# Storing the first tile of a gated linear unit by rows instead of in one piece

## The chip, the cores and the metric

The kernel runs on one core of a Trainium2 chip. The metric is device time in microseconds (us) of one launch. Before the change it is 933.2 us. A timed run is called slow when it lies over 1.5% above the fastest of the same kernel; the others are called fast.

## The reference

```python
def reference(x):                       # x: 8192 x 8192, float32
    a, b = np.split(x, 2, axis=-1)
    return a * (1 / (1 + np.exp(-b)))   # 8192 x 4096, float32
```

It reads 268 MB, writes 134 MB, and does one sigmoid and one product per output element.

## The kernel before

The matrix is cut into 32 tiles of 256 rows; each of the 128 partitions holds two neighbouring rows. There are two input slots (64 KB per partition each) and two output slots (32 KB each). SyncE issues one load per tile, ScalarE takes the sigmoid in place, VectorE multiplies into the output slot, and ScalarE issues the store. Only the first and the last tile are computed in quarters: row 0's two halves, then row 1's.

```python
    for i in range(n_tiles):
        ...
        load = nc.sync.dma_start(out=xs[i % SLOTS], in_=x_t[i])
        ...
        if 0 < i < n_tiles - 1:
            parts = [(slice(0, R), slice(0, half))]
        else:
            w = half // 2
            parts = [
                (slice(r, r + 1), slice(c * w, (c + 1) * w)) for r in range(R) for c in range(2)
            ]
        ...
        for k, (r, c) in enumerate(parts):
            b = rows[:, r, 1, c]
            sig = nc.scalar.activation(out=b, in_=b, func=SIG)
            mul = nc.vector.tensor_mul(out=packed[:, r, c], in0=rows[:, r, 0, c], in1=b)
            ...
            by_sigmoid = i % 2 == 1 and len(parts) == 1
            implied(mul, *(s for s in old["stores"] if by_sigmoid or s not in freed))
            if by_sigmoid:
                for s in freed:
                    tc.add_manual_dep(sig.ins, s.ins.name, DEP, reason="frees the output slot")
            ...
            if i == n_tiles - 1 and k > 0:
                store(chunks[k - 1])
        store(chunks[-1] if i == n_tiles - 1 else slice(0, R * half))
```

The words that follow: a DMA engine moves data between HBM (the main memory) and SBUF (the memory on the chip), and a core has 16 of them. By the traces' packet records, each of the 16 moves eight packets of 64 KB of a load and eight of 32 KB of a store, and then one *semaphore packet* of 4 bytes; when all 16 of these are through, the transfer has landed and the instruction that waits for it may start. A *ring* is the list of packets that loads, or stores, have waiting on an engine; it runs empty when the next transfer is issued too late.

`implied` takes away a dependency that follows from others. `freed` are the stores that must have landed before the output slot is written again: tile k waits for store k-2. In odd tiles the sigmoid does this waiting (`by_sigmoid`), in even ones the product.

## Time and profile before

| What | Value | Where from |
|---|---|---|
| time, median of 3 runs | 933.2 us (933.03 to 933.31) | timed runs |
| span of the profiled run | 931.7 us | page |
| one tile of 8.39 MB in and 4.19 MB out | 29.0 us | loads' semaphore packets in the trace |
| ScalarE per tile, VectorE per tile | 7.03 us, 8.69 us | groups of instructions |

A tile needs 29.0 us of the DMA engines and 15.7 us of computing, which lies beside other transfers. The windows view has one line per stretch (from:to, length, busy time and count of each engine, granted clock, share of the DMA engines, GB/s); its line for 200 to 490 us of the kernel before gives the steady rate:

```profile
200.00:490.00 290.00, 86.95 (x11) 70.31 (x10) 0.00 (x0) 1.00 1.00 434
```

The waits view (who waited for what: us in total, times, longest) of the kernel before has no wait for a store at all; the input is always what comes last:

```profile
ACT x_sb L68 <- DMA x_sb<-in_x_dram: 694.4, 32, 22.3
DVE o_sb L69 <- ACT x_sb L68: 647.1, 33, 23.9
```

### The profile page before, as it was taken

The page shows a single profiled execution, that of the slowest core. Times are in us where ns is not written, and L with a number is a line of the kernel's source. Part 1 is how long each engine was busy: PE and PEld are TensorE (multiplying, and loading weights), DVE is VectorE, ACT ScalarE, POOL GpSimd, SP SyncE. Part 2 cuts the span into 40 slices and gives each one's busy share as a digit, 9 for nine tenths or more (in the row PEclk, how much of TensorE's full clock was granted, in tenths as well). Part 3 has the DMA queues.
Part 4 walks back from the last instruction along what each step waited for, and adds up shares of the span by engine and source line. Part 5 has one row for each costly group of instructions (what it writes and reads, how often), then busy time and mean ns, then how long its engine had stood idle before and what let it go on. Part 6 is the DMA issues. An engine that isn't in the chain of part 4 may idle for free.

```text
span 931.7 us, 247 instructions
## 1 busy us (share of the span) xinstructions
DVE 278.7 (30%) x38; ACT 227.1 (24%) x39; POOL 0.2 (0%) x4
## 2 busy tenths in 40 slices
DVE  0333213333133331233312333123331233312333
ACT  1323330233311333113331133311333113332033
POOL 0000000000000000000000000000000000000000
DMA  9999999999999999999999999999999999999999
GB/s 405 428 450 428 422 456 405 450 428 428 450 418 438 428 436 442 428 428 450 447 408 428 442 459 428 413 460 411 450 428 425 453 408 447 428 428 450 425 430 405
DMA packets 9649, 402.67 MB, mean 432 GB/s; under 512 B 1072, under 2 KB 1072, under 8 KB 1072
## 3 DMA queue, kind: packets, MB, share of 16 engines
q1 hardware_dynamic: 4608, 268.44, 66.6%
q10 hardware_dynamic: 5040, 134.22, 33.4%
q14 instruction: 1, 0.01, 0.0%
HBM read 268.44 MB, written 134.22 MB: 432 GB/s over the span
## 4 chain that ended last, share of the span: by engine, by line
DMA 73%; DVE 15%; ACT 12%; issue 0%; ACTq 0%
DMA x_sb<-in_x_dram 73%; DVE o_sb L69 15%; ACT x_sb L68 12%; ACTq L62 0%; ACTq L68 0%
## 5 line engine op out<-in xcount | busy, mean ns | idle before, releaser
L69 DVE TENSOR_TENSOR o_sb<-x_sb 128x8192 f32<-128x8192 f32 (+1 forms) x38 | 278.7, 7344 | 647.1 <-ACT x_sb L68 647.1
L68 ACT ACTIVATE x_sb<-x_sb 128x8192 f32<-128x8192 f32 (+1 forms) x38 | 225.8, 5952 | 695.6 <-DMA x_sb<-in_x_dram 694.4
L68 ACT ACT_TABLE_LOAD x1 | 1.3, 1283 | 0.8 <-PEq L188 0.8
L188 POOL MEMSET const-bfloat16-1.0<- 128x1 bf16 x1 | 0.1, 102 | 0.0
L188 POOL MEMSET const-uint8-127<- 128x1 uint8 x1 | 0.1, 102 | 0.0
L188 POOL MEMSET const-float32-0.0<- 128x1 f32 x1 | 0.1, 99 | 0.2 <-issue 0.2
L188 POOL MEMSET const-float32-1.0<- 128x1 f32 x1 | 0.1, 99 | 0.0
## 6 DMA issues: line engine op xcount, KB each, us to landing
out_dram<-o_sb ACTq DMA_DIRECT2D x31, 4096.0 KB, 34.7
out_dram<-o_sb ACTq DMA_DIRECT2D x4, 1024.0 KB, 5.6
x_sb<-in_x_dram SPq DMA_DIRECT2D x32, 42.2
```

Source lines behind the costliest of these rows:

```text
L68: sig = nc.scalar.activation(out=b, in_=b, func=SIG)
L69: mul = nc.vector.tensor_mul(out=packed[:, r, c], in0=rows[:, r, 0, c], in1=b)
L188: nc = _bacc.Bacc("TRN2", target_bir_lowering=False, num_devices=1)
```

## The change

The intent is to start storing earlier: row 0 of the first tile leaves as soon as its two products are done.

```diff
             if i == n_tiles - 1 and k > 0:
                 store(chunks[k - 1])
-        store(chunks[-1] if i == n_tiles - 1 else slice(0, R * half))
+            if i == 0 and r.start > 0 and c.start == 0:
+                store(slice(0, half))
+        if i == 0:
+            store(slice(half, R * half))
+        else:
+            store(chunks[-1] if i == n_tiles - 1 else slice(0, R * half))
```

## The prediction

> **What bounds the kernel now.** I read the page's slices first, then its queues and DMA issues, then the chain of waits, then the timeline of the first two tiles, and last the DMA view of one tile's time in the middle.
>
> ```profile
> DVE  0333213333133331233312333123331233312333
> ACT  1323330233311333113331133311333113332033
> ...
> DMA  9999999999999999999999999999999999999999
> ...
> q1 hardware_dynamic: 4608, 268.44, 66.6%
> q10 hardware_dynamic: 5040, 134.22, 33.4%
> ...
> HBM read 268.44 MB, written 134.22 MB: 432 GB/s over the span
> ...
> DMA x_sb<-in_x_dram 73%; DVE o_sb L69 15%; ACT x_sb L68 12%; ACTq L62 0%; ACTq L68 0%
> ...
> out_dram<-o_sb ACTq DMA_DIRECT2D x31, 4096.0 KB, 34.7
> out_dram<-o_sb ACTq DMA_DIRECT2D x4, 1024.0 KB, 5.6
> x_sb<-in_x_dram SPq DMA_DIRECT2D x32, 42.2
> ```
>
> The compute engines are busy in one to three tenths of each slice; the 16 DMA engines in nine tenths or more of every one, the first and the last included. The two queues' packet times add up to 66.6 + 33.4 = 100% of the engines' span. So the time is bytes over rate: 402.66 MB at 432 GB/s is 932 us. The chain of waits gives 15% to VectorE and 12% to ScalarE, and it would be easy to read 27% to be won there; but while those instructions run, the DMA engines move the other slot's load and the previous store. The chain tells which event released which, not which resource was short.
>
> The timeline of the start shows what the change touches:
>
> ```profile
> 21.95 7.31 ACT L68 ACTIVATE x_sb<-x_sb 128x2048 f32<-128x2048 f32 x4 [19.89 <-DMA x_sb<-in_x_dram]
> 23.89 8.90 DVE L69 TENSOR_TENSOR o_sb<-x_sb 128x2048 f32<-128x2048 f32 x4 [23.89 <-ACT x_sb L68]
> 32.82 0.38 ACTq L62 DMA_DIRECT2D out_dram<-o_sb  x1
> 44.80 7.03 ACT L68 ACTIVATE x_sb<-x_sb 128x8192 f32<-128x8192 f32 x1 [15.53 <-DMA x_sb<-in_x_dram]
> 51.86 8.69 DVE L69 TENSOR_TENSOR o_sb<-x_sb 128x8192 f32<-128x8192 f32 x1 [19.07 <-ACT x_sb L68]
> 60.58 0.36 ACTq L62 DMA_DIRECT2D out_dram<-o_sb  x1
> ```
>
> Load 1 was issued at the start, right behind load 0, so it streams from 21 to 44 us whatever the store does. There is no hole for an earlier store to fill. In the windows view, 0 to 33 us (loads alone) moves 413 GB/s with the start-up in it, and 45 to 103 us (both kinds) 434 GB/s.
>
> In the middle, 129 to 158 us, the DMA view says:
>
> ```profile
> DMA packets 288, 12.58 MB, mean 434 GB/s; under 512 B 32, under 2 KB 32, under 8 KB 32
> ...
> q1 hardware_dynamic: 144, 8.39, 66.7%
> q10 hardware_dynamic: 144, 4.19, 33.5%
> ```
>
> In 29 us exactly one load and one store pass. Per engine that is 8 data packets of 64 KB and 8 of 32 KB, and one small semaphore packet each. The packet records give 2.42 us for a 64 KB packet, 1.21 for 32 KB and 0.31 for 8 KB: the time goes with the bytes, with almost nothing fixed per packet. 8 x (2.42 + 1.21) = 29.0 us. Read engine by engine, they alternate strictly: a load packet, a store packet; a semaphore packet takes a turn too.
>
> **What the Trainium skill says.** "DMA: Bandwidth & Descriptors", section "Queues, rings and completion order", says that each DMA engine goes round-robin between the queue rows that have work, packet by packet. The trace agrees (144 against 144 packets). Its "Specifications" give a fabric ceiling of 435 GB/s; the 434 GB/s measured here sits at it, so nothing that reorders transfers can raise the rate. "Perfetto Trace Analysis", section "DMA Optimizations", says that splitting DMAs may help "If DMA engines are generally idle"; here they are not, so by that page the split has nothing to win.
>
> **The change part by part.**
> 1. *Issue times.* Sigmoids are 1.9 us and multiplies 2.29 us each. The second product ends at 23.89 + 2.29 + 2.2 = 28.4 us; row 0's store is issued at 28.4 instead of 32.8, 4.4 us earlier. It stands in ScalarE's order after the third sigmoid (done at 27.5) and before the fourth, which now starts near 28.8 instead of 27.4 and ends at 30.7. The fourth product starts then instead of at 30.5: row 1's store and load 2 leave at about 33.1, 0.25 us later. Load 2 isn't needed before load 1 has landed at 44, so this costs nothing.
> 2. *Packets.* Store 0 becomes 16 packets of 16 KB per engine (estimate from the row above: 0.61 us) for 8 of 32 KB, and one more semaphore packet (0.009 us in the records). 16 x 0.61 - 8 x 1.21 is under 0.1 us. Sum: +0.1 us.
> 3. *Turns.* This is the part that really moves something. While store 0 is in flight, a round is 2.42 + 0.61 = 3.03 us instead of 3.63: the load still gets a full 64 KB turn, the store only 16 KB. Before, the store's first packet came 6 us after its issue (38.9; the engine finished its current load packet and the next, which was stretched from 2.4 to 3.3 us). With the same lag the first 16 KB packet comes at 34.0. Then load 1's last three packets take turns with it: 34.0 + 3 x 3.03 + 0.61 = 43.7 us for load 1's semaphore, the same as now (43.7): two turns of 32 KB or four of 16 KB have gone in between. Load 1 lands at 44.8 in both. Store 0 has then 11 packets of 16 KB left. Load 2's eight rounds cost 8 x 3.03 = 24.2 us, so it lands near 68.9 instead of 73.65. Load 3 meets three more 16 KB turns and one semaphore turn, then four 32 KB ones: its semaphore at 94.6 and landing at 95.5 instead of 102.8. The loads run ahead by 7 us, and the stores fall behind by the same bytes.
> 4. *The new wait.* Store 0's last semaphore falls at 80.1 (landing 81.0); the third tile's product, ready at 75.9, waits for its output slot and ends at 89.7 (now 89.4). Store 1, issued at 60.6, gets its first turn at 82.5 and its last semaphore at 109.1, landing at 110.0 instead of 95.3. Tile 3 is odd: its sigmoid waits for store 1. It starts at 110.1, 14 us after its load has landed, and load 5 and store 3 go out at 110.1 + 7.03 + 8.69 = 125.9, where now it is 118.7. Load 4 is through at 122.5, so the load ring is empty for about 4 us. In that time the store ring still holds three or four packets of store 2, until 128.5. Load 5's packets can come from 126.9 (one microsecond after issue, as for the first load). So the DMA engines stay busy, with 1.6 us in hand; the loads fall back by those store packets.
> 5. *Afterwards.* I followed the turns to tile 7: store k-2 lands about 3.6 us after load k, odd tiles wait for it that long, and both rings always hold work. 29.0 us per tile as before.
> 6. *The end.* Some 4 store packets per engine more are left when the last load has landed (4 x 1.21 = 4.8 us), and that load is earlier by about the same. Now the last quarter's store is issued at 925.8, and the store queue works without a gap until 930.8. After the change the compute tail of 11 us (925.8 - 914.7) starts near 910 and ends near 921, while stores keep the engines busy to the same end.
>
> Sum: +0.1 us of packets, and a waking load ring at 126 us, which may stretch a packet by up to 0.9 us as the first store's did. I take half of that: +0.5 us. 933.2 + 0.5 = 933.7.
>
> **The rivals.**
> A. *The earlier store shortens the kernel by its 4.4 us* (0.5%), 928.8. For it: the chain has the first tile's compute in it. Against: no slice is idle, so 4.4 us would need a rate above 434 GB/s.
> B. *The slot wait drains both rings.* Step 4 has only 1.6 us in hand at 126 us; if the store's queue runs out first, or the wait recurs as a bubble at each odd tile, the cost is 1 to 3 us once (936), or 15 times 1 us (948). Against the recurrence: after the first time 5 to 8 store packets are left whenever a load is issued late.
> C. *The small packets cost.* 16 KB at half the efficiency would add 10 us x 1 = 10 us. Against: 8 KB packets take 0.31 us, a quarter of the 32 KB time.
> D. *The late tail.* If the last tile's products waited for store 29, the last stores would be late. One packet of it is left then, 1.2 us plus about 1 us to land; the first sigmoid takes 1.9 us. No cost.
>
> **Range and chances.** The three runs before span 0.3 us. Downward I see only spread, 0.5 to 1 us. Upward there are B's single bubble and differences between chips: 932.7 to 935.3. Two per cent are 18.7 us; only a recurring bubble with much more than 1 us per odd tile would reach it: 0.01 for slower, 0.005 for faster.
>
> **What would show it right or wrong.** Right: row 0's issue near 28.4; 144 packets more in q10 and 100% of DMA time; load 2 landing near 69 and load 3 near 95.5; a new line in the waits, ScalarE's sigmoid (or VectorE's product) released by a store, near 3 to 4 us per odd tile with one of 14; the store's median landing longer than 34.7 by some 10 us; the last sigmoid near 910. Wrong: DMA digits under 9 near 126 us or at the end, a period other than 29.0 us, or load landings that don't move. A faster time with unchanged DMA rate would sink the whole reading.

## The result

| | median | runs |
|---|---|---|
| before | 933.23 us | 6 runs, 933.03 to 933.78 |
| changed | 935.51 us | 933.74, 933.99, 934.19, 936.83, 941.03, and one slow run of 960.4 |

The ratio of the fast runs is 1.0027 (95% interval 1.0006 to 1.0048). Such a ratio is the mean time of one kernel's fast runs over that of the other's of the same rounds, so it isn't quite the ratio of the medians. It is a small loss, 0.2 us outside my range. The median of 935.51 takes in the slow run: that of the five fast ones is 934.19, inside my range, and that of all nine fast runs, with those of the repeat below, 935.44. More striking than its size is the spread: the six runs of the kernel before lie within 0.8 us, the five fast ones of the changed kernel within 7.3 us.

From the page of the changed kernel (the profiled run took 936.83 us, span 935.4), the lines that answer to those of before:

```profile
DMA  9999999999999999999999999999999999999998
...
q1 hardware_dynamic: 4608, 268.44, 66.6%
q10 hardware_dynamic: 5184, 134.22, 33.3%
...
out_dram<-o_sb ACTq DMA_DIRECT2D x30, 4096.0 KB, 42.2
out_dram<-o_sb ACTq DMA_DIRECT2D x2, 2048.0 KB, 39.3
out_dram<-o_sb ACTq DMA_DIRECT2D x4, 1024.0 KB, 8.1
```

The store queue has its 144 packets more (5184 instead of 5040) and still the same share of the time, so the smaller packets cost nothing that shows. The stores take 42.2 us from issue to landing instead of 34.7, and the last four 8.1 instead of 5.6.

The timeline of the changed kernel (start, length, engine, instruction; in brackets what ended the idle time before it):

```profile
28.49 0.37 ACTq L62 DMA_DIRECT2D out_dram<-o_sb  x1
...
33.18 0.36 ACTq L62 DMA_DIRECT2D out_dram<-o_sb  x1
45.98 7.03 ACT L68 ACTIVATE x_sb<-x_sb 128x8192 f32<-128x8192 f32 x1 [15.16 <-DMA x_sb<-in_x_dram]
...
70.16 7.03 ACT L68 ACTIVATE x_sb<-x_sb 128x8192 f32<-128x8192 f32 x1 [17.15 <-DMA x_sb<-in_x_dram]
82.36 8.69 DVE L69 TENSOR_TENSOR o_sb<-x_sb 128x8192 f32<-128x8192 f32 x1 [20.62 <-DMA out_dram<-o_sb]
...
111.20 7.03 ACT L68 ACTIVATE x_sb<-x_sb 128x8192 f32<-128x8192 f32 x1 [34.01 <-DMA out_dram<-o_sb]
...
126.99 0.36 ACTq L62 DMA_DIRECT2D out_dram<-o_sb  x1
```

Row 0 leaves 4.3 us earlier than the whole store did. The third tile's product (82.36) and the fourth tile's sigmoid (111.20) now wait for a store. The waits view says the same for the whole run:

```profile
ACT x_sb L68 <- DMA x_sb<-in_x_dram: 357.7, 17, 22.0
ACT x_sb L68 <- DMA out_dram<-o_sb: 327.3, 14, 34.0
DVE o_sb L69 <- DMA out_dram<-o_sb: 20.6, 1, 20.6
```

Where the time went in this run shows in the windows view of the changed kernel:

```profile
120.00:128.00 8.00, 6.96 (x1) 0.60 (x1) 0.00 (x0) 1.00 1.04 451
128.00:146.00 18.00, 8.69 (x1) 6.42 (x1) 0.00 (x0) 1.00 1.00 402
146.00:900.00 754.00, 223.29 (x26) 182.75 (x26) 0.00 (x0) 1.00 1.00 434
...
931.00:935.40 4.40, 0.00 (x0) 0.00 (x0) 0.00 (x0) 1.00 0.39 166
```

Between 128 and 146 us the rate is 402 GB/s (18 us x 32/434 = 1.3 us lost) with the DMA share still at 1.00: packets took longer, and no engine stood idle. After 931 us the engines are on average only 39% busy: some are done and others aren't.

The packet records show both. They don't name the engine, so I put packets into 16 sequences by letting each start where another ended. One of them, in the changed kernel (start, L = load or S = store with KB, or sem for a semaphore packet, length):

```
120.10 L64 2.42 | 122.51 S32 1.21 | 123.72 Lsem 0.01 | 123.73 S32 1.21 | 124.94 S32 1.21
126.15 S32 1.21 | 127.36 S32 1.21 | 128.57 Ssem 0.01 | 128.57 L64 3.13 | 131.70 S32 1.21
...
153.53 S32 1.21 | 154.74 L64 2.42 | 157.15 S32 1.21 | 158.36 Lsem 0.01 | 158.37 Ssem 0.01
```

The load ring ran empty at 123.7, as worked out beforehand; stores alone followed to the end of store 2; at 128.6 both rings started anew, with a load packet of 3.1 us instead of 2.4. Three things show in the records:
- The load packets between 120 and 160 us are 1.4 us longer per engine in sum, and not equally on all engines. The spread between the first and the last engine's semaphore packet of one transfer was 0.6 us in the kernel before, from start to end. Here it is 1.8 us from the first store on and 3.1 us after 128 us. In this run it doesn't shrink again; each engine has the same sixteenth of every transfer to move.
- The first engine ends at 932.0 us instead of 930.7, and the last at 935.1 instead of 931.4. Of the profiled 3.7 us, 1.3 are longer packets on the fastest engine and 2.4 are spread.
- From there on load and store end together (158.36 and 158.37). In the kernel before, store k ended 7.3 us earlier than load k+2. I call this difference, measured on the first engine to get there, the **distance**: -7.3 us before, 0.0 after. It turned out to be what matters most.

### The profile page after: what moved, and what is told of

Same layout as the page of the kernel before. It is cut to its first block, busy times and chain, and to the rows that moved or that the text cites. A ratio compares the mean times of both kernels' runs of the same rounds, so it can differ in the third digit from the quotient of the medians.

```text
span 935.4 us, 249 instructions
## 1 busy us (share of the span) xinstructions
DVE 278.7 (30%) x38; ACT 227.1 (24%) x39; POOL 0.2 (0%) x4
## 3 DMA queue, kind: packets, MB, share of 16 engines
q10 hardware_dynamic: 5184, 134.22, 33.3%
## 4 chain that ended last, share of the span: by engine, by line
DMA 72%; DVE 15%; ACT 12%; issue 0%; ACTq 0%
DMA out_dram<-o_sb 63%; DVE o_sb L69 15%; ACT x_sb L68 12%; DMA x_sb<-in_x_dram 9%; ACTq L62 0%
## 6 DMA issues: line engine op xcount, KB each, us to landing
out_dram<-o_sb ACTq DMA_DIRECT2D x30, 4096.0 KB, 42.2
```

## The experiments

All runs are compared with the kernel before on the same chip in the same rounds; its medians lay between 933.2 and 933.9 us.

### The changed kernel again

No edit.

> The changed kernel once more, unaltered, to see its spread (933.7 to 941.0 us in five fast runs, one of 960). Theory W (waking rings leave the 16 DMA engines out of step for good, and the slowest sets the end): median 934 to 937 us, the spread of the last semaphore packets between engines again 2 to 4 us where the kernel before has 0.6, rising at about 34 and 128 us. Rival P (the 16 KB packets or the extra semaphore packet cost time by themselves): a fixed 0.1 us, no spread, 933.3. Rival C (a disturbed chip made the first six runs slow): median within 0.3 us of the kernel before.

Measured: 935.08, 935.44, 935.66, 937.43 us, and slow runs of 963.85 and 966.44; ratio of the fast runs 1.0025 (1.0012 to 1.0038). So the loss and the lack of repetition are real, and the rivals "16 KB packets cost a fixed amount" and "a disturbed chip" fall. The profile fell on a slow run (965 us): its tiles take 30.2 us, and a load packet of nearly every engine is stretched twice per tile. No conclusion rests on the slow runs alone; the sign comes back below in fast ones.

### The product waits instead of the sigmoid

```diff
-            by_sigmoid = i % 2 == 1 and len(parts) == 1
+            by_sigmoid = False
```

> The changed kernel, but in every tile the product, not the sigmoid, waits for the output slot. Worked by turns: load 5 leaves near 120 us instead of 127, before load 4 is through at 122.5 to 123.7, so the load ring never runs empty. Theory W: the step of the spread between engines at 128 us is gone (1.8 us stays instead of 3.1), no stretched packets near 128 us, time 933.5 to 934.5, and the loads stay 7 us ahead (last load through near 906). If only the first wake at 34 us matters: no gain against the changed kernel (934 to 937). Rival P: same as the changed kernel.

Measured: 933.71 us (933.50 to 934.49, no slow run), ratio 1.0003 (0.9990 to 1.0015). The waits view of this kernel:

```profile
ACT x_sb L68 <- DMA x_sb<-in_x_dram: 687.0, 32, 22.3
DVE o_sb L69 <- DMA out_dram<-o_sb: 601.2, 30, 20.8
```

Every tile's product now waits for a store, 30 times instead of once, and yet the loss is gone. The last load was through at 906.5 us, as expected. The store is still early, split and in 16 KB packets, so none of these costs by itself. What differs is that the load ring doesn't run empty at 123.7 and that the distance stays at +14.5 us. At the end the spread is 1.9 us; it grew slowly from 430 us on.

### An attempt to split without being early

```diff
-            if i == 0 and r.start > 0 and c.start == 0:
-                store(slice(0, half))
         if i == 0:
+            store(slice(0, half))
             store(slice(half, R * half))
```

> Both row stores issued one after the other when all four products are done: split but not early. By turns: first store packet at 38.9, load 2 lands near 68 us, store 0 lands near 86, load 4 leaves near 94.5 while load 3 is through at 92, so the load ring wakes once near 96 us. Theory W: about the cost of the change itself, 933.7 to 936 us, with a step of the spread between engines near 96 us. Rival E (the earlier issue is what costs, as it starts the store stream in the middle of load 1): 933.2 to 933.5. Rival P: 933.3.

This didn't make what I wanted: row 0's store still waits for its own two products alone, and was issued at 28.3 us. Only its place in ScalarE's order moved, behind the fourth sigmoid. Measured: fast runs of 933.82, 933.91, 935.45 and 935.90, slow ones of 962.1 and 966.8, ratio 1.0013 (1.0000 to 1.0026); first semaphores within 0.5 us of the changed kernel's up to 128 us. Two of the four fast runs lie above every run of the kernel before (934.37 at most), so some loss stays without the delayed fourth sigmoid; whether that sigmoid has a part in it, the interval leaves open. About lateness the run says nothing.

### An empty load ring alone

```diff
         now["loads"].append(load)
+        if i == 5:
+            tc.add_manual_dep(load.ins, load_before.ins.name, DEP, reason="late on purpose")
+        load_before = load
```

(in the kernel before)

> The kernel before with one addition: load 5 also waits until load 4 has landed, so that the load ring runs empty once, near 131 us, for about 2 us, while the store ring still holds five packets per engine. No store is split or early. Theory W: stretched load packets near 133 us and a lasting rise of the spread between engines by 1 us or more, time 934 to 936. If an empty ring costs nothing while the other ring has work, as a count of bytes says: 933.2 to 933.5, spread 0.6 to the end.

Measured: 933.34 us, ratio 1.0000 (0.9988 to 1.0012). I expected a microsecond or more, and was wrong: the load ring ran empty near 131 us, load 5 left at 131.7, and the packets were stretched by only 0.05 us per engine, while the loads' spread went from 0.6 to 2.0. The last stores came within 0.5 us of each other all the same. The store ring was still full here, whereas in the changed kernel it was just running out too. So a ring that runs empty does not cost by itself. The distance afterwards is -9.5 us.

### An attempt to store late in one piece

The whole store 0 was written behind the second tile's sigmoid in the source.

> Store 0 whole, as in the kernel before, but issued later (after the second tile's sigmoid, near 48 us instead of 32.8): neither split nor early. By turns: load 2 is through near 65, store 0 lands near 81, store 1 near 110, load 5 and store 3 leave together near 126 while load 4 is through near 123, as in the changed kernel. Theory L (the store stream falling behind the loads makes the load ring run empty once; load 5 and store 3 then start together and from there each load ends with the store two tiles back, and it is this lock that makes runs of 935 to 966 us possible): median 934 to 937, one or two of six runs over 945, last load and store semaphores of a tile within 1 us of each other. Rival E/P (splitting or the early issue costs): 933.2 to 933.6 and no slow run, as of the kernel before.

Measured: 933.24 us, ratio 0.9995. The run tells nothing: the order that was built still had the store ahead of that sigmoid (issued at 32.72 us), so it is the kernel before once more. The runs with a held-back store below replace it.

### Load 1 in halves

```diff
-        load = nc.sync.dma_start(out=xs[i % SLOTS], in_=x_t[i])
-        implied(load, *old["loads"], *old["sigs"])
-        now["loads"].append(load)
+        for c in [slice(0, n_cols), slice(n_cols, R * n_cols)] if i == 1 else [slice(0, R * n_cols)]:
+            load = nc.sync.dma_start(out=xs[i % SLOTS][:, c], in_=x_t[i, :, c])
+            implied(load, *old["loads"], *old["sigs"])
+            now["loads"].append(load)
```

(in the changed kernel)

> The changed kernel, but load 1 comes in two row halves, so its packets are 32 KB and the turns give row 0's store half the bytes of the load, as in the steady state. By turns: load 1 through near 45, load 2 near 69, store 0's second semaphore near 72, load 3 near 97.5, store 1 near 101; load 5 leaves near 118 while load 4 is through near 126, so the load ring never runs empty; the store's end follows the load's by 3 to 4 us. Theory L: no slow run, 933.3 to 934.0. Rival E/P: as the changed kernel, 935 and slow runs, since the store is still split and early.

The turns came as worked out (load 1 through at 45.2, load 2 at 69.6, load 3 at 98.0, store 1 at 99.7 to 101.9, no empty ring), and the time didn't: fast runs of 936.97, 936.98, 939.03, 944.59 and 947.64, one slow of 959; ratio 1.0077 (1.0042 to 1.0111). So there is a loss, and a larger one, without an empty ring, and the empty ring can't be the only cause. What this kernel has in common with the changed one is the small distance: in its profile, which fell on the slow run, half of the engines are at 0 and the other half at +3.6 us.

### Breaking the distance in mid-run

```diff
+        if i == 17:
+            tc.add_manual_dep(load.ins, load_before.ins.name, DEP, reason="late on purpose")
+        load_before = load
```

(in the changed kernel)

> The changed kernel, but load 17 also waits until load 16 has landed: the loads fall behind there once, so that from about 510 us on stores end some 10 us or more before the loads two tiles later, and the lock is broken. Theory L: if a run is slow, its load packets are stretched and its tiles take 30.2 us up to about 510 us and 29.0 us after it, so slow runs are at 945 to 952 us and none is over 955; fast runs 934 to 937. Rival R (a slow run is slow because of the chip or the buffers, whatever the phase): slow runs stay slow to the end, 960 to 967.

Measured: 934.67 to 939.01, median 936.34, ratio 1.0029 (1.0016 to 1.0041), none of six runs over 940. That fits, but two slow runs in six might also just not have come, so it decides little. The break itself stretched packets by 1.1 us per engine.

The profiled run (935.34 us) shows one thing more. Up to 480 us it is the changed kernel; its load ring ran empty at 123.5, and load 5 and store 3 started together at 128.3. Yet the load packets between 120 and 160 us were not longer (0.0 us per engine, against 1.4 in the first profile), and the spread stayed at 0.5 us. So the restart doesn't always cost. Five profiled executions pass through it. The time from the issue of load 5 to the end of store 2 on the first engine, and how many of the 16 engines then had a first load packet of over 2.5 us:

| run | time in hand | engines with a stretched packet | load packets, 120 to 160 us, longer by |
|---|---|---|---|
| the changed kernel | 1.5 us | 16 | 1.4 us |
| the same again (slow run) | 1.8 us | 16 | 1.2 us |
| load 7 late (below) | 2.5 us | 4 | 1.0 us |
| split, not early (slow run) | 2.8 us | 4 | 0.7 us |
| load 17 late (this one) | 2.8 us | 1 | 0.0 us |

Load 5 is issued late where the spread of the first store is large (1.8 and 1.4 us in the first two, 0.4 to 0.8 in the others), since it waits for the last engine. It looks as if the restart costs the more, the less time the load has in hand; five executions suggest it, and no run varied this time alone.

### The distance alone, in steps

Now the kernel before, with nothing split and nothing early: store 0 is held back by 2, 4, 6 or 8 small activations on a spare tile (1.3 us each). Each 2.4 us lets one more load packet pass before the store stream starts, so the distance grows by one round of 3.63 us (a load packet of 2.42 and a store packet of 1.21 us).

```diff
+    junk = pool.tile([P, 1320], fp32, name="junk")
+    nc.vector.memset(junk, 0.0)
 ...
+        if i == 0:
+            for _ in range(2):           # 2, 4, 6, 8
+                wait = nc.scalar.activation(out=junk, in_=junk, func=SIG)
+                tc.add_manual_dep(wait.ins, mul.ins.name, DEP, reason="late on purpose")
         store(chunks[-1] if i == n_tiles - 1 else slice(0, R * half))
+        if i == 0:
+            tc.add_manual_dep(now["stores"][0].ins, wait.ins.name, DEP, reason="late on purpose")
```

> The kernel before with its store 0 whole, held back by two small activations on a spare tile (about 2.5 us, one load packet). One load packet more passes before the store stream starts, so each store ends 3.6 us earlier than the load two tiles later instead of 7.3 us earlier. Nothing is split, no ring runs empty. Theory F (what costs is how far a store's packets lie from those of the load that runs with it: ends within about 4 us of each other are bad, 7 us or more apart are good; splitting, the early issue and an empty ring only matter as they set this distance): between the two, 933.3 to 936. Rivals E/P (split or early issue) and L (the load ring running empty): 933.2 to 934.0, as the kernel before.

> As the last, held back by about 5 us: loads and stores end together (distance 0), as in the changed kernel from 128 us on, but here without an empty ring and without a split. Theory F: 934 to 937 in the median, one or two of six runs over 940, load packets stretched twice per tile in such a run. Rivals E/P and L: 933.2 to 934.0, no slow run.

> Held back by about 7.5 us: each store ends 3.6 us after the load, as in the run with load 1 in halves. Theory F: 936 to 945 in the median, load packets stretched once per tile. Rivals E/P and L: 933.2 to 934.0.

> Held back by about 10 us: each store ends 7.3 us after the load. Theory F: near 933.3 to 935, better than the run held back by 7.5 us, if the distance must be small to do harm. If lagging stores as such do harm, whatever the distance: over 940. Rivals E/P and L: 933.2 to 934.0.

| store 0 issued at | distance | median | ratio of the fast runs (95%) |
|---|---|---|---|
| 32.8 (before) | -7.3 us | 933.92 us | |
| 35.35 | -3.6 us | 933.75 us | 0.9999 (0.9985 to 1.0014) |
| 37.98 | 0.0 us | 934.18 us, one fast run of 943.76 | 1.0019 (0.9991 to 1.0048) |
| 40.70 | +3.6 us | 953.09 us (953.00 to 953.34, 4 runs) | 1.0206 (1.0193 to 1.0219) |
| 43.51 | +7.2 us | 933.47 us | 0.9997 (0.9984 to 1.0010) |

This is the clearest result. Holding the store back by one more packet costs 19 us in every run, and yet another packet gives all of it back. My theory had expected 936 to 945 at +3.6 us, so it had the place right and the size too small. The windows view of the kernel with +3.6 us, and one line of the kernel with +7.2 us:

```profile
200.00:490.00 290.00, 83.47 (x10) 66.81 (x10) 0.00 (x0) 1.00 1.00 425
560.00:890.00 330.00, 95.75 (x12) 77.32 (x11) 0.00 (x0) 1.00 1.00 425
```

```profile
200.00:490.00 290.00, 86.87 (x11) 70.29 (x10) 0.00 (x0) 1.00 1.00 434
```

At +3.6 us the DMA engines are fully busy (1.00), at 425 GB/s instead of 434. In its packet records from 200 to 900 us, put into sequences as above, about six in ten second packets of a load and eight in ten third ones took over 2.5 us; of the fifth to eighth none. In the kernel before it was one of all. At distance 0 the profiled run (a fast one) shows no such stretching; there it comes in some runs only. The rivals "split", "early" and "empty ring" all expected 933 to 934 here.

### Is it the addresses?

Loads and stores might meet at bad addresses in HBM. "DMA: Bandwidth & Descriptors", section "Latency and other measured facts", reports large losses for certain power-of-two row pitches, with channel aliasing as an unverified inference; its figures begin at a pitch of 512 KB, and here a partition's rows are 64 KB apart in the input and 32 KB in the output. So I kept the timing of the +3.6 us kernel and wrote each tile to other rows (wrong result):

```diff
-            ins = nc.scalar.dma_start(out=out_t[i, :, cols], in_=os[i % SLOTS][:, cols])
+            top = P * R * ((i or n_tiles - 1) - 1) + R * 16 if i < n_tiles - 1 else P * R * i   # 0, 1, 16, 64
+            wrong = out[top : top + P * R, :].rearrange("(p r) m -> p (r m)", r=R)
+            ins = nc.scalar.dma_start(out=wrong[:, cols], in_=os[i % SLOTS][:, cols])
```

> Wrong result on purpose. The run held back by 7.5 us (953 us), each tile from 1 to 30 written one whole tile (4 MB) lower, nothing else changed: the control for the next three. Theory H (addresses in HBM collide) with a pattern that repeats within 4 MB: 950 to 956. Theory T (timing alone): 950 to 956. Under 940 would already mean addresses, with a longer pattern.

> Wrong result on purpose. As the control, and all rows 32 KB (one partition's store packet) further. Theory H: if an engine's next packet is the next partition, this makes the addresses meet as at another distance, so the time changes clearly, to under 940. Theory T: 950 to 956 as the control.

> Wrong result on purpose. As the control, and all rows 16 x 32 KB = 512 KB further. Theory H: if the engines take partitions in turn, so that an engine's next packet is 16 partitions on, this is the shift by one packet: under 940. Theory T: 950 to 956.

> Wrong result on purpose. As the control, and all rows 64 x 32 KB = 2 MB further, half a tile. Theory H: likely to differ from the control unless the pattern repeats within 2 MB. Theory T: 950 to 956.

Measured: 952.61, 953.07, 953.03 and 952.52 us (ratios 1.0207, 1.0214, 1.0212, 1.0207). Moving the output by one tile (4 MB), and by 32 KB to 2 MB against that, changes nothing, so addresses of the output that collide with the input's are not the cause at any of these shifts.

### Is it the place of the wait?

The product-waits edit in the +3.6 us kernel, and the late load 17 in the same kernel:

> The run held back by 7.5 us (953.1), but in every tile the product, not the sigmoid, waits for the output slot; both rings stay filled, so each store should still end 3.6 us after the load. Theory F (the distance): 950 to 955. Theory S (a sigmoid held up by a store is what goes with the slow runs): 933 to 936.

> The run held back by 7.5 us (953.1), but load 17 also waits until load 16 has landed. From about 520 us on stores then end 10 us or so before the loads. Theory F: tiles of 29.4 to 29.8 us with stretched load packets before that, of 29.0 us without after it; half of the 19.8 us is lost, and about a microsecond at the break: 943 to 946. Rival (a run's or buffer's property, set at the start): 952 or more, stretched to the end.

Measured: 953.20 us (ratio 1.0214) and 944.64 us (942.48 to 945.30, ratio 1.0118). With the sigmoid's wait gone and the distance kept (72.57 - 68.94 = 3.63 us), all of the loss stays. With the waits kept and the distance broken in mid-run, the loss stops there, in one and the same execution:

```profile
200.00:490.00 290.00, 82.88 (x10) 66.81 (x10) 0.00 (x0) 1.00 1.00 426
560.00:890.00 330.00, 100.55 (x12) 77.32 (x11) 0.00 (x0) 1.00 1.00 434
```

It is 426 GB/s before the break and 434 after it. A property of the run, of the chip or of the buffers' place would have stayed to the end; and the 953 us came on three chips.

### Restart or distance, in the changed kernel

The late-load edit at `i == 7` in the changed kernel.

> The changed kernel, and load 7 also waits until load 6 has landed, near 190 us: the restart at 128 us stays, the distance of 0 lasts for a tile or two only, from about 220 us on stores end some 10 us before the loads. If the restart costs the 2 us and the distance makes the long runs: 934.5 to 936.5, no run over 940. If the distance of 0 costs both: 933.3 to 934.3, no run over 940. If runs over 940 still appear, the distance isn't what makes them.

Measured: 935.60 to 938.42, median 937.41, ratio 1.0036 (1.0022 to 1.0049); no run over 940. The windows view:

```profile
128.00:146.00 18.00, 8.69 (x1) 5.33 (x1) 0.00 (x0) 1.00 1.02 428
146.00:186.00 40.00, 8.69 (x1) 7.03 (x1) 0.00 (x0) 1.00 1.00 417
186.00:220.00 34.00, 8.69 (x1) 7.03 (x1) 0.00 (x0) 1.00 1.02 422
220.00:900.00 680.00, 201.90 (x24) 168.71 (x24) 0.00 (x0) 1.00 1.00 434
```

The low rates lie between the restart and the break; from 220 us on it is 434 GB/s. That the long runs don't come fits the distance: with the break in load 17 it is none over 940 in 11 runs, against 4 of the 12 of the changed kernel. These are few runs, so it is a hint. That a loss stays fits its rise in the first 100 us after the load ring ran empty, but the break adds its own part (packets stretched by 1.4 us per engine from 180 to 200 us), which may be why it is above the 936.5 I had allowed. In its profile the load packets are 1.0 us longer per engine from 120 to 160 us and 0.8 us from 160 to 180, at distance 0 and before the break. How much of the ordinary 2 us is the restart and how much the first tiles at distance 0, this run doesn't separate; at distance 0 without a restart (the second step above), five of six runs were at 933.85 to 934.25.

## Why the prediction was wrong

**What bounds the kernel** and the **rate** in the middle: right as far as it went. The engines were busy in every slice but the last, and the fast profiled run moved 434 GB/s in the steady part. What I concluded from it was too much: "nothing that reorders transfers can raise the rate" holds in all 18 experiments (none was faster), but I let it stand for "can't change the rate". At a distance of +3.6 us the rate is 425 with busy engines. A DMA share of 100% says that packets are in progress, and nothing about how long each takes. (One reading of the page was loose: VectorE's first slice has a 0, not one to three tenths.)

**Steps 1 to 3** (issue times, packets, turns): right. Row 0 left at 28.49 (28.4 worked out), row 1 at 33.18 (33.1). The first engine's semaphores for loads 1, 2 and 3 came at 43.8, 68.0 and 94.6 (43.7, 67.9 and 94.6 by the turns), the two of store 0 at 55.9 and 80.1, and store 1's at 109.1 (109.1). The landings are some 1.2 us later than I said, since I added the spread of the kernel before (0.6 us) and it was 1.8. That the first of these times is right to 0.1 us is partly luck: the first 16 KB packet came at 33.5 and not at 34.0, and the load packets beside it took 2.5 to 2.9 us and not 2.42, which made up for it.

**Step 4** (the new wait): the times are right to 1.1 us, its conclusion failed. Sigmoid 3 started at 111.2 (110.1), load 5 left at 127.0 (125.9), the load ring was empty, and the store ring bridged the gap exactly to the end of store 2. What failed is "Load 5's packets can come from 126.9 (one microsecond after issue, as for the first load)". In the five executions of the table above they came 1.5 to 2.8 us after the issue, and only when store 2 had ended on that engine; and with 1.5 us in hand all 16 engines stretched that packet.

**Step 5** failed. I had written "store k-2 lands about 3.6 us after load k, odd tiles wait for it that long, and both rings always hold work. 29.0 us per tile as before". As load 5 had no turn before the end of store 2, load 5 and store 3 set off together, so the distance became 0 and not 3.6, and I gave the distance no price. Measured prices in the kernel before: 0 costs nothing or, in one of six runs, 10 us; +3.6 costs 19 us. At that price the kernel would have been near 953, had the turns fallen as I worked them out (an inference; this was not run). That 933.7 is so near is luck: the error in step 4 kept the kernel off the distance of step 5.

**Step 6** (the end) failed with it. I expected the last load some 5 us early, and it was 1.3 us early on the first engine (912.4 against 913.7); the last sigmoid started at 915.95, not near 910. One of my signs of being wrong came true: the DMA digit of the last slice is 8, since some engines were done while the slowest set the end.

**The sum.** The mis-sized term is the waking load ring, "I take half of that: +0.5 us". I had taken one engine's sequence for all sixteen. In the profiled run the load packets from 120 to 160 us were 1.4 us longer on average, and not equally, and the last engine set the end: +3.7 us in span. Other executions paid 0.0 to 1.2 us there (the table above), so the term has no fixed size. Over the fast runs of the first six, the loss is 0.27% or 2.5 us.

**The rivals.** B (both rings drain) named the right place and nearly the right size, 936, by another mechanism: nothing drained, packets were stretched. It also feared a loss at each odd tile; this exists at a distance of +3.6 us, where every tile takes longer. C (small packets) fell: the store queue's share is unchanged. A and D didn't occur.

**What stays open.** Why two or three load packets are stretched when a store ends a few microseconds after a load is not settled. It isn't the output's address at the shifts tried, not the place of the wait, not the split, and not a slow chip. It goes with the distance, that is, with the order of packets within the engines. The buffers' places in SBUF, the input's addresses and the sizes of the packets in the steady state were not varied. For the changed kernel's own loss it is shown that it goes when the product waits instead of the sigmoid; which share falls to the restart and which to distance 0 is argued. All six slow runs fell on kernels at distance 0, or 0 and +3.6; that the distance makes them is not shown.

## What to carry to other kernels

In this kernel, which is bound by DMA, an earlier store moved no end; what it moved was the phase between the load and the store stream, and that phase stayed until something broke it. So compare the DMA rate and single packets' durations, and the ends of the two streams, before and after such a change, and be suspicious when runs no longer repeat. When a change of a few microseconds at the start loses time, shift the first store by one or two packets before discarding the idea: here one packet was worth 19 us.

## What the Trainium skill lacked or had wrong

- "DMA: Bandwidth & Descriptors" gives rates for one stream and says of several that they interleave ("Issuing engines are not separate DMA queues"). It lacks that the rate of a load and a store stream depends on their phase: 953.1 us against 933.5 for one packet's shift, 425 against 434 GB/s with all engines busy.
- The same page, "Queues, rings and completion order": its round-robin is confirmed (load and store packets alternate in the records). It lacks that a semaphore packet takes a turn (after each load's semaphore packet a second store packet follows), and that a turn here was one packet of 64 KB against one of 32 or 16: beside 16 KB store packets load 2 took 24.2 us instead of 29.0.
- The same page, "Latency and other measured facts", has a first byte after about 0.6 us. With idle engines the first packet began 1.0 us after the start of its issue here (which itself took 0.37 us, so the two may not measure the same); with engines busy on another ring the first store packet came 6 us after its issue, after two more load packets of 2.4 and 3.4 us.
- The same page, "Bandwidth", says that for HBM to SBUF the HBM side (about 358 GB/s) binds. That doesn't fit one core alone, as the 425 GB/s of its own table shows; here reads and writes together ran at 434 GB/s.
- No page found says that the 16 engines can fall out of step within a run and stay so: spreads of 0.6 us in the kernel before, 3.1 us in the changed one, each to the end.
